# The head of a pooling and state-space decoder step: rows scaled in place before plain transposes, dt from the unsplit h, modulation in quarters, and a new order of loads and operations

## The chip, the cores and the metric

The kernel runs on one core of one Trainium2 chip. The time is that of one execution on the device, in microseconds (us), from the first to the last instruction of the core with what lies around it; a kernel's time is the median of its runs. All data are float32. Products that must be accurate are made as three passes over split numbers: an operand is split into a rounded high part (type fp32r) and the rest, the low part, and high x high, high x low and low x high are summed.

## The reference, cut to what matters

One layer of a hybrid decoder for 1024 prompt tokens and 8 x 8 sample tokens, 1088 rows in all. The change touches only the beginning:

```python
mod = jax.nn.silu(c) @ w_ada + b_ada                  # c: 1 prompt row + 8 sample rows
shift, scale, gate = jnp.split(mod, 3, axis=-1)       # 1024 each
h = rmsnorm(x, norm_g) * (1 + scale[:, None]) + shift[:, None]
proj = h @ w_in                                       # 1024 -> 8224 columns
u_pool, z_pool, z_ssm, xbc, dt_raw, g_raw = jnp.split(proj, SPLITS, axis=-1)
...                                                   # pooling, convolution, state space, gates
m = gates[..., :D_MODEL] * p + gates[..., D_MODEL:] * s
x = x + gate[:, None] * (m @ w_o)
```

`rmsnorm` divides each row of x by its root mean square. `w_ada` has 1024 x 3072 numbers: shift, scale and gate each take a third.

## The kernel before, in words

**The whole.** The projection h @ w_in is the first half of the program. After a head, columns come in 31 pairs of 128, each pair by one step of Strassen's scheme: seven products instead of eight, each of 24 matmuls (L595 to L597; two halves of 272 columns, four row blocks of the contraction, three passes). The state-space chunks and the output products follow, and a short tail of normalised output rows (L1954 to L1996). A program records instructions in an order written by hand; where `in_line` is called, that order is kept on every engine.

**The head (`first`, L838 to L999).** Its order is written out; engines take their instructions strictly in that order, and so does the queue of SyncE (SP), which issues nearly all loads.

1. The nine row blocks of x (128 rows each, 64 in the last) are loaded, then squared and summed (`x_square`; four on ScalarE, the 64 sample rows among them, five on VectorE), and 1/rms comes from a root and a reciprocal (`x_root`, `x_unit`). `x_unit` builds a diagonal matrix of 1/rms per block (L219).
2. `x_turn` (L223 to L233) multiplies each 128 x 128 piece of x by that diagonal matrix on TensorE (PE): the result is the piece turned and scaled, tokens along the free axis. There are 72 such products in ordinary float32, which the trace shows as two records each. `x_copy` brings them from PSUM into `tf[k]`, k = 0 to 7 being the eight blocks of 128 features. Tokens are cut in three blocks of 256, 384 and 448 columns, `BLK`, here called blocks 0, 1 and 2.
3. `ada_load`, `ada_mm`, `ada_out`, `ada_end`: the shift and scale thirds of w_ada (8 MB) are loaded in three parts (features k = 0 and 1, 2 and 3, and 4 to 7 of both), multiplied by silu(c) in four column groups of the array at once (L277), turned (L292) and finished with bias and norm weight into `md` (L296 to L299).
4. `h_make` (L309 to L335): from `tf[k]` and `md` it makes h in `tf[k]` itself (`L325` on ScalarE, `L327` on VectorE), its high part `hh_` (`L323`, `L332`, ScalarE) and low part `hl_` (`L315`, VectorE); the 64 sample columns have a shift and scale of their own (L330, L331, called the tail below).
5. `products`: the first pair of gate columns is made by plain three-pass products of h with two weight tiles of 512 columns' worth, loaded in halves (`w_first`: k < 4 and k >= 4), block by block (L866 to L868). `done` applies the sigmoid and stores the result.
6. `dt_block` (L720 to L731): the 32 columns of dt, as two sums, over the high and over the low parts of h, each in ordinary float32.
7. `gate_load`, `gate_mm`: the gate third of w_ada (4 MB, eight loads) for the end of the kernel; `gate_end` stores it.
8. `combine` (L471 to L519): the sums and differences of quarters of h for Strassen's scheme (S1 to S4), each split in high and low parts. The first pair of the scheme ("first pair" below) starts while these are being made.

**Buffers.** PSUM has 8 banks: three in pool `psA` (`PA`) and five in `psB` (`PB`). SBUF pools hand a buffer on when its last reader is done: 8 of tag `G` (blocks of w_ada, then h of k >= 4), 5 of `rawA` (scratch and raw weights of pairs), 3 of `raw`, 3 of `R`.

Of the kernel before, what the change touches and what calls it, by code (L numbers as in the profile page):

```python
# [20 lines left out]
P = 128  # L21
D = 1024
# [31 lines left out]
def tile_pool_ssd_step(  # L54
# [86 lines left out]

    c9 = const([P, KT, NB + 1], "c9")
# [42 lines left out]
    xr = []  # L185
# [4 lines left out]
    dg = []  # L190
# [3 lines left out]
    def x_load(i):  # L194
        n = P if i < 8 else NS
        xt = R([P, D]) if i == 8 else xbig[i // 4][:, i % 4, :D]
        load(xt[:n], x_prompt[0, i * P:(i + 1) * P, :] if i < 8 else x_sample.rearrange("b t d -> (b t) d"))
        xr.append((xt, n))
# [13 lines left out]
    def x_unit(a, b):  # L212
        n = xr[a][1]
        V.reciprocal(rs[:n, a:b], rs[:n, a:b])
        if not dg:
            dg.append(R())
        for i in range(a, b):
            n = xr[i][1]
            V.tensor_scalar(dg[0][:n, i * P:i * P + n], ident[:n, :n], rs[:n, i:i + 1], None, ALU.mult)  # L219
# [3 lines left out]
    def x_turn(g3, k):  # L223

        if g3 == 0:
            tf[k] = tfp.tile([P, T], F32, tag="tf", name=nm("tf"), bufs=8)
        px = PB()
        c = 0
        for i in range((0, *XG)[g3], XG[g3]):
            xt, n = xr[i]  # L230
            mm(px[:, c:c + n], xt[:n, k * P:(k + 1) * P], dg[0][:n, i * P:i * P + n], start=True, stop=True)
            c += n
        return g3, k, px, c  # L233
# [9 lines left out]
    def x_turns(g3, ks):  # L243
        for k in ks:
            x_copy(x_turn(g3, k), nc.scalar if k % 2 else V)


    PARTS = ((0, 2), (2, 4), (4, 8))
    pm, wraw, wtile = [None] * 3, {}, {}
    md = const([P, 16, 9], "md")  # L250

    def ada_load(part, k):
        a, b = PARTS[part]
        w = (b - a) * P
        if part == 0:
            if k == 0:
                wtile[0] = Y4(hp, F32)
            t = wtile[0][:, k // 2, :D]
        else:
            if part == 2 or k % 2 == 0:  # L260
                wtile[part, k] = G((P, D))
            t = wtile[part, k if part == 2 else k - k % 2]
        if part == 2:
            load(t, w_ada[8 + k])
        else:
            if k % 2 == 0:
                load(t, w_ada[4 * part + k // 2])
            t = t[:, k % 2 * 512:k % 2 * 512 + 512]
        wraw[part, k] = t.rearrange("p (s c) -> p s c", s=2)
# [17 lines left out]
    def ada_end(part, mr):  # L287
        a, b = PARTS[part]
        ni = (b - a) // 2
        ps = PB()  # L290
        for i in range(ni):
            nc.tensor.transpose(ps[:, i * P:(i + 1) * P], mr[:, i * P:(i + 1) * P], ident)  # L292
# [16 lines left out]
    def h_make(g3, ks):  # L309

        o, w = BLK[g3]
        e = min(o + w, SEQ) - o

        def low(k):
            V.tensor_tensor(hl_[k][:, o:o + w], tf[k][:, o:o + w], hh_[k][:, o:o + w].bitcast(F32), ALU.subtract)  # L315
        for k in ks:
            if hh_[k] is None:
                hh_[k], hl_[k] = h_tile(k, 0), h_tile(k, 1)
            t = tf[k][:, o:o + w]
            hi = hh_[k][:, o:o + w]  # L320
            sc, sh = md[:, 8 + k], md[:, k]
            if e == w:
                act(hi, t, AF.Identity, scale=sc[:, 0:1], bias=sh[:, 0:1])  # L323
            if k % 2:
                act(t[:, :e], t[:, :e], AF.Identity, scale=sc[:, 0:1], bias=sh[:, 0:1])  # L325
            else:
                V.tensor_scalar(t[:, :e], t[:, :e], sc[:, 0:1], sh[:, 0:1], ALU.mult, ALU.add)  # L327
            if e < w:
                ts_ = t[:, e:w].rearrange("p (b i) -> p b i", i=8)
                V.tensor_tensor(ts_, ts_, sc[:, 1:9].unsqueeze(2).to_broadcast([P, NB, 8]), ALU.mult)  # L330
                V.tensor_tensor(ts_, ts_, sh[:, 1:9].unsqueeze(2).to_broadcast([P, NB, 8]), ALU.add)  # L331
                act(hi, t, AF.Copy)  # L332
            if k > ks[0]:
                low(k - 1)
        low(ks[-1])  # L335


# [133 lines left out]
    def combine():  # L471
        L_, R_ = slice(0, HF), slice(HF, T)

        big = []

        def parts(src, hi, lo):
            act(hi, src, AF.Copy)
            V.tensor_tensor(lo, src, hi.bitcast(F32), ALU.subtract)

        def room(lst, k):  # L480
            if lst is S1:
                lst[k] = (hs.tile([P, 2, HF], F32R, tag="sq", name="S1", bufs=1) if k == 3 else R((P, 2, HF), F32R))
            else:
                if k == 0:
                    big.append(Y4(hs).rearrange("p k (j n) -> p k j n", j=2))
                lst[k] = big[-1][:, k]

        def part(lst, k, src):
            room(lst, k)
            parts(src, lst[k][:, 0], lst[k][:, 1])  # L490

        def low(k):
            V.tensor_tensor(S2[k][:, 1], tf[k][:, L_], S2[k][:, 0].bitcast(F32), ALU.subtract)
        for k in range(4):
            a, b = tf[k], tf[k + 4]
            room(S2, k)
            V.tensor_tensor(b[:, R_], a[:, R_], b[:, R_], ALU.add)
            V.tensor_tensor(a[:, R_], a[:, L_], a[:, R_], ALU.subtract)
            V.tensor_tensor(a[:, L_], b[:, R_], a[:, L_], ALU.subtract)
            act(S2[k][:, 0], a[:, L_], AF.Copy)  # L500
            if k:
                low(k - 1)
# [1579 lines left out]
```

## Time and profile before

| | |
|---|---|
| median of 3 runs | 1238.93 us (1238.75 to 1239.34) |
| profiled execution, span | 1238.8 us, clock 0.999 |
| PE busy | 1213.9 us, 98% |
| VectorE / ScalarE / GpSimd busy | 909.2 / 692.8 / 678.0 us |
| moved by DMA | 243.25 MB, mean 196 GB/s |

The profiled execution's own span, 1238.8 us, lies within 0.2 us of the median, so sums made in the trace stand for the time as they are. In the views, PE is TensorE, PEld its weight loads, DVE VectorE, ACT ScalarE, POOL GpSimd and SP SyncE; L231 is a line of the kernel before, and an idle time is followed by what ended it. PE records overlap (one ends after the next has begun), so the price of a matmul is the distance of two starts, not its length.

### The profile page before, as it was taken

How to read it: one execution, taken by the hardware profiler on the slowest of the kernel's cores; microseconds unless marked ns; L12 is line 12 of the kernel's file. 1: busy time of each engine (PE TensorE's matmuls, PEld its weight loads, DVE VectorE, ACT ScalarE, POOL GpSimd, SP SyncE). 2: the span in 40 equal slices, each digit the busy share in tenths (PEclk: the TensorE clock that was granted, in tenths of full speed). 3: DMA queues.
4: the chain of work that ended last, by engine and by line, in shares of the span. 5: the costliest groups of instructions: out<-in, count | busy, mean ns of one | idle time of the engine just before them, and what ended most of it. 6: DMA issues, size and time to landing. Idle time of an engine off the chain costs nothing. (4 is left out here: it accounts for less than half of the span.)

```text
span 1238.8 us, 25381 instructions
## 1 busy us (share of the span) xinstructions
PE 1213.9 (98%) x9364; PEld 1145.0 (92%) x9364; DVE 909.2 (73%) x1579; ACT 692.8 (56%) x1611; POOL 678.0 (55%) x555
## 2 busy tenths in 40 slices
PE   6999999999999999999999999999999999999997
PEld 6779999999999999999898899999999999999786
DVE  4796688985989588975867775787767879666543
ACT  4665356565566556554554454877877768432111
POOL 1006669768898877774444465364565557456000
PEclk9999999999999999999999999999999999999999
DMA  9726445755556554453877775998665676485431
GB/s 363 290 99 226 145 161 148 188 190 170 164 173 208 158 168 146 169 179 114 251 248 211 231 223 183 329 306 298 192 203 176 195 228 198 143 296 167 153 111 51
DMA packets 183916, 243.25 MB, mean 196 GB/s; under 512 B 40808, under 2 KB 116912, under 8 KB 183792
## 3 DMA queue, kind: packets, MB, share of 16 engines
q1 hardware_dynamic: 132128, 167.90, 42.9%
q10 hardware_dynamic: 51664, 73.72, 17.6%
q8 instruction: 74, 1.21, 0.4%
q14 instruction: 50, 0.41, 0.1%
HBM read 166.96 MB, written 74.62 MB: 195 GB/s over the span
## 5 line engine op out<-in xcount | busy, mean ns | idle before, releaser
L166 POOL TENSOR_TENSOR wlo<-rawA,whi 128x512 fp32r<-128x512 f32 x120 | 187.5, 1569 | 143.1 <-DVE wlo L166 67.7
L166 POOL TENSOR_TENSOR wlo<-raw,whi 128x512 fp32r<-128x512 f32 x92 | 150.2, 1640 | 126.1 <-ACT whi L163 119.9
L360 PE MATMUL mm<-Y,whi 128*128 128x352 f32 (+1 forms) x480 | 160.1, 334 | 0.6
L361 PE MATMUL mm<-Y,whi 128*128 128x352 f32 (+1 forms) x480 | 157.1, 327 | 0.4 <-DVE Y L1485 0.4
L362 PE MATMUL mm<-Y,wlo 128*128 128x352 f32 (+1 forms) x480 | 157.1, 327 | 0.0
L595 PE MATMUL mm<-Y,whi 128*128 128x272 f32 x496 | 144.5, 292 | 1.0 <-ACT whi L163 0.8
L597 PE MATMUL mm<-Y,wlo 128*128 128x272 f32 x496 | 143.5, 290 | 1.3 <-DVE wlo L166 0.8
L596 PE MATMUL ps<-Y,whi 128*128 128x272 f32 x496 | 143.2, 289 | 0.0
L595 PE MATMUL ps<-Y,whi 128*128 128x272 f32 x496 | 142.8, 288 | 0.0
L597 PE MATMUL ps<-Y,wlo 128*128 128x272 f32 x496 | 142.8, 288 | 0.0
L596 PE MATMUL mm<-Y,whi 128*128 128x272 f32 x496 | 142.5, 287 | 0.0
L1031 DVE SCALAR_TENSOR_TENSOR GA<-GA,cvT,GA 128x1112 f32<-128x1112 f32 x72 | 128.4, 1786 | 0.7 <-ACT GA L1028 0.5
L163 ACT ACTIVATE whi<-rawA 128x512 fp32r<-128x512 f32 x125 | 77.8, 626 | 90.4 <-PE ps L596 51.1
L163 ACT ACTIVATE whi<-raw 128x512 fp32r<-128x512 f32 x96 | 58.7, 626 | 83.0 <-DVE raw L540 38.2
L595 PEld LDWEIGHTS mm<-Y,whi 128*128 128x128 f32 x496 | 93.6, 189 | 4.6 <-issue 2.4
L597 PEld LDWEIGHTS mm<-Y,wlo 128*128 128x128 f32 x496 | 93.1, 188 | 3.0 <-DVE wlo L166 1.2
L595 PEld LDWEIGHTS ps<-Y,whi 128*128 128x128 f32 x496 | 93.4, 188 | 1.7 <-issue 0.8
L596 PEld LDWEIGHTS mm<-Y,whi 128*128 128x128 f32 x496 | 93.5, 188 | 0.8 <-issue 0.6
L360 PEld LDWEIGHTS mm<-Y,whi 128*128 128x128 f32 x480 | 90.2, 188 | 4.1 <-DVE G L1861 2.3
L596 PEld LDWEIGHTS ps<-Y,whi 128*128 128x128 f32 x496 | 93.3, 188 | 0.2
L597 PEld LDWEIGHTS ps<-Y,wlo 128*128 128x128 f32 x496 | 93.2, 188 | 0.0
L361 PEld LDWEIGHTS mm<-Y,whi 128*128 128x128 f32 x480 | 90.2, 188 | 2.6 <-DVE Y L1485 0.9
(422 smaller groups left out, 3727.0 us busy)
## 6 DMA issues: line engine op xcount, KB each, us to landing
rawA<-in_w_in SPq DMA_DIRECT2D x62, 512.0 KB
dec<-acs_d SPq DMA_DIRECT2D x32, 512.0 KB
xbc<-GA ACTq DMA_DIRECT2D x24, 512.0 KB
xb<-xbc SPq DMA_DIRECT2D x32, 384.0 KB
pw<-in_w_ssm_out ACTq DMA_DIRECT2D x32, 256.0 KB
ws<-ph ACTq DMA_DIRECT2D x32, 256.0 KB
ws<-pw SPq DMA_DIRECT2D x32, 256.0 KB
hs<-in_state_turned SPq DMA_DIRECT2D x32, 256.0 KB
```

The lines of the kernel that those rows point to most:

```text
L163: ins = act(hi[:, :, :ncols], raw[:, :, :ncols], AF.Copy)
L166: (eng or nc.gpsimd).tensor_tensor(lo[:, :, :ncols], raw[:, :, :ncols], hi[:, :, :ncols].bitcast(F32), ALU.subtract)
L360: mm(ps[:, :n], a, rh[k][:, o:o + n], start=(k == 0), stop=False)
L361: mm(ps[:, :n], a, rl[k][:, o:o + n], start=False, stop=False)
L362: mm(ps[:, :n], b, rh[k][:, o:o + n], start=False, stop=(k == nk - 1))
L595: mm(p, hi, ah, start=(k == 0), stop=False)
L596: mm(p, hi, al, start=False, stop=False)
L597: mm(p, lo, ah, start=False, stop=(k == 3))
L1031: V.scalar_tensor_tensor(d[:, :n], rp[:, k:k + n], cvT[:, 24 * k + mc:24 * k + mc + 1], d[:, :n], ALU.mult, ALU.add)
```

## The change

All of it is in the head; the instructions from the second pair on stand in the same order on every engine. In parts:

- `x_unit` no longer builds diagonal matrices. `x_scale` multiplies the rows of x by 1/rms in place (five blocks and the sample block on VectorE, three on ScalarE), and `x_turn` is a transpose against the identity. The sample block is filled to 128 rows with zeros and turned whole.
- 32 products of the identity with itself (`hot`) stand at the start of PE's order. ScalarE loads the root's table before it needs it. The sigmoid results go through `rawA` buffers.
- Shift and scale come in four parts of two features each.
- `h_make` is cut into single steps (`h_high`, `h_line`, `h_low`, `h_tail`, `h_copy`), some of which read PSUM directly; `combine` likewise. Four of the eight tail steps go to GpSimd, and so do three of the weight splits of the second half of the head and of the first pair.
- dt is made from h in `tf`, before the sums overwrite it: one sum instead of two.
- The order of everything in `first` is written out anew.
- The loads of the pooling weights and the loads of the next pairs' weights stand later in SP's order, and splits of the pairs that follow are held behind the last steps of the first pair's preparation (`tc.issue_after(held[...])`).

```diff
+    def x_scale(i, eng):
+        xt, n = xr[i]
+        if eng is None:
+            act(xt[:n], xt[:n], AF.Copy, scale=rs[:n, i:i + 1])
+        else:
+            eng.tensor_scalar(xt[:n], xt[:n], rs[:n, i:i + 1], None, ALU.mult)
...
-            mm(px[:, c:c + n], xt[:n, k * P:(k + 1) * P], dg[0][:n, i * P:i * P + n], start=True, stop=True)
+            nc.tensor.transpose(px[:, c:c + P], xt[:, k * P:(k + 1) * P], ident)
...
-    PARTS = ((0, 2), (2, 4), (4, 8))
+    PARTS = ((0, 2), (2, 4), (4, 6), (6, 8))
...
+    def h_line(g3, k, eng, src=None):
...
+        if eng is V:
+            V.tensor_scalar(t, u, sc, sh, ALU.mult, ALU.add)
+        else:
+            act(t, u, AF.Identity, scale=sc, bias=sh)
...
-    def dt_block(w, i):
+    def dt_mm(w, i):
         o, n = BLK[i]
-        ps = PA()
+        ps = dtp[i] = PA()
         for kk in range(2):
-            for part in (hh_, hl_):
-                for r in range(4):
-                    k = 4 * kk + r
-                    mm(ps[32 * r:32 * r + 32, :n], w[:, k, :], part[k][:, o:o + n].bitcast(F32),
-                       start=(kk == 0 and part is hh_), stop=(kk == 1 and part is hl_))
+            for r in range(4):
+                k = 4 * kk + r
+                mm(ps[32 * r:32 * r + 32, :n], w[:, k, :], tf[k][:, o:o + n], start=(kk == 0), stop=(kk == 1))
...
-            add(b11)
+            with tc.issue_after(held["act"]):
+                add(b11)
...
+        def hot(n):
+            for _ in range(n):
+                mm(banks[1, 0][:, :P], ident, ident, start=True, stop=True)
+
+        hot(20)
+        x_load(1)
+        x_load(0)
+        x_load(7)
...
-        x_turns(0, range(2))
...
+        products(1, range(7, 8))
...
+        next(opening, None)
+        sums_c(0)
...
```

On SP the loads at the start stand like this before (`Y_128` and `Y_129` hold x, `R_226` the sample rows, `Y_228` the first part of w_ada, `G_` the second, `raw_` the first halves of the first weights):

```order
L197 DMA Y_128<-in_x_prompt 128x1024 x4
L197 DMA Y_129<-in_x_prompt 128x1024 x4
L197 DMA R_226<-in_x_sample 64x1024
L267 DMA Y_228<-in_w_ada 128x1024 x3
L846 DMA raw_232<-in_w_first 128x512
L846 DMA raw_234<-in_w_first 128x512
L267 DMA Y_228<-in_w_ada 128x1024
L267 DMA G_237<-in_w_ada 128x1024
```

And after (`Y_129` and `Y_130` hold x, `R_245` the sample rows, `Y_248` the first part):

```order
L199 DMA Y_129<-in_x_prompt 128x1024 x2
L199 DMA Y_130<-in_x_prompt 128x1024 x3
L199 DMA R_245<-in_x_sample 64x1024
L258 DMA Y_248<-in_w_ada 128x1024 x2
L199 DMA Y_129<-in_x_prompt 128x1024
L199 DMA Y_130<-in_x_prompt 128x1024
L199 DMA Y_129<-in_x_prompt 128x1024
L258 DMA Y_248<-in_w_ada 128x1024 x2
L258 DMA G_256<-in_w_ada 128x1024
```

Two blocks of tokens of block 0 and the four of block 2 come first, two loads of w_ada are put ahead of the three row blocks of block 1, and the first weights come after the first part of w_ada.

Later on SP, the second halves of the first weights (`raw_578`, `raw_584`), the gate third (`R_`, `gk_`) and the last part of shift and scale (`G_574`, `G_580`) stand like this after; ahead of this piece are all of x, 14 blocks of w_ada's first two thirds and the two first halves:

```order
L789 DMA R_527<-in_w_ada 128x1024
L789 DMA R_529<-in_w_ada 128x1024
L258 DMA G_574<-in_w_ada 128x1024
L789 DMA R_576<-in_w_ada 128x1024
L818 DMA raw_578<-in_w_first 128x512
L258 DMA G_580<-in_w_ada 128x1024
L789 DMA gk_582<-in_w_ada 128x1024
L818 DMA raw_584<-in_w_first 128x512
L516 DMA rawA_586<-in_w_in 128x1024
L516 DMA rawA_588<-in_w_in 128x1024
L376 DMA cvT<-in_conv_vecs 128x120
```

Before, in the same place, the loads of the pooling weights (`pwt_`) stood between the two second halves (`raw_550`, `raw_552`), and the gate third came behind all of this:

```order
L846 DMA raw_550<-in_w_first 128x512
L748 DMA pwt_1290<-in_pool_w 128x128
L748 DMA pwt_2444<-in_pool_w 128x128
L748 DMA pwt_3919<-in_pool_w 128x128
L846 DMA raw_552<-in_w_first 128x512
L264 DMA G_554<-in_w_ada 128x1024
L264 DMA G_556<-in_w_ada 128x1024
L264 DMA G_558<-in_w_ada 128x1024
L264 DMA G_560<-in_w_ada 128x1024
```

The pooling weights left this place; four loads of the gate third moved ahead of the last weights.

On PE, at the end of the head, dt's products over high (`Y_463`, `G_727`) and low parts (`Y_464`, `G_728`, `G_733`) and the last four of the gate third stood right ahead of the first pair (L595):

```order
L727 MATMUL mm_955<-G_728,dtw 32x448
L727 MATMUL mm_955<-G_733,dtw 32x448
L823 MATMUL ps_794<-R_799,scT 32x256 x4
L823 MATMUL ps_794<-R_805,scT 32x256 x4
L823 MATMUL ps_794<-R_835,scT 32x256 x4
L823 MATMUL ps_794<-gk_841,scT 32x256 x4
L595 MATMUL mm_1009<-Y_463,whi_946 128x272
```

After, they read `tf` and stand among the products of blocks 1 and 2; the last of those (`ps_596`) now stand right ahead of the first pair (L563):

```order
L845 MATMUL ps_596<-G_863,whi_740 128x448
L846 MATMUL ps_596<-G_863,wlo_741 128x448
L847 MATMUL ps_596<-G_864,whi_740 128x448
L563 MATMUL mm_1064<-Y_490,whi_902 128x272
L564 MATMUL mm_1064<-Y_491,whi_902 128x272
L565 MATMUL mm_1064<-Y_490,wlo_903 128x272
```

What follows the first pair's first product on PE is a long row of like matmuls in both.

More of the change, by code (lines that the diff above doesn't have):

```diff
@@ new lines, in first @@
+        tt[1, 4] = x_turn(1, 4)
+        h_low(0, 0)
+        h_high(1, 1)
+        ada_mm(1, 3)
+        ada_load(3, 2)
+        gate_load(1)
+        gate_load(3)
+        w_lo(1, 0, V)
+        x_copy(tt[1, 5], nc.scalar)
+        ada_mm(1, 4)
+        x_copy(tt[1, 0], V)
+        products(0, range(0, 1))
+        h_copy(0)
+        h_line(1, 1, V)
+        h_high(1, 0)
+        ada_mm(1, 5)
+        h_low(2, 0)
+        ada_mm(2, 0)
+        x_copy(tt[1, 4], nc.scalar)
+        ada_mm(1, 6)
@@ new lines, in first @@
+        h_line(1, 0, V)
+        ada_mm(2, 1)
+        h_line(2, 1, None)
+        ada_mm(1, 7)
+        ada_load(3, 6)
+        gate_load(0)
+        w_load(1, 1)
+        ada_load(3, 4)
+        gate_load(2)
+        w_load(0, 1)
+        b11, b12, b21, b22 = light[0][0]()
+        for _ in late_loads():
+            pass
+        h_low(1, 1)
+        products(2, range(0, 1))
+        mr[1] = ada_out(1)
+        h_low(1, 0)
+        h_copy(1)
+        h_high(0, 1)
+        h_low(2, 1)
+        pt_[1] = ada_turn(1, mr[1])
@@ L958, in first @@
+        ada_mm(3, 5)
+        gate_mm(1)
+        h_high(0, 4)
+        h_low(2, 4)
+        ada_mm(3, 6)
+        h_high(1, 4)
+        gate_mm(2)
+        gate_load(6)
+        gate_load(5)
+        h_line(0, 4, V)
+        ada_mm(3, 7)
+        w_hi(0, 1)
+        h_low(0, 5)
+        gate_mm(3)
+        gate_load(7)
+        gate_load(4)
         dtw = dt_w()
-        run, (wz, wst) = light[0][1], light[0][0]()
         bg = gate_bias()
-        for k in range(4):
-            gate_load(k)
@@ L983, in first @@
-        dt_block(dtw, 2)
-        next(sums)
-        for k in range(4, 8):
-            gate_mm(k)
-        gate_end(bg)
-        next(late, None)
-        def hook(n):
-            if n in (0, 2):
-                next(wst)
-            if n < 2:
-                next(sums)
-            if n in (3, 4):
-                next(wst)
-                next(sums)
-        run(wz, hook)
+        h_low(0, 4)
+        h_line(1, 4, None)
+        products(1, range(2, 3))
+        w_lo(0, 1, V)
+        mr[3] = ada_out(3)
@@ new lines, in first @@
+        h_high(1, 7)
+        h_low(0, 6)
+        h_line(0, 7, V)
+        h_line(1, 6, None)
+        products(0, range(6, 7))
+        pw_diff(3)
+        h_line(1, 7, None)
+        products(1, range(5, 6))
+        h_low(0, 7)
+        h_copy(7)
+        h_low(1, 7)
+        h_line(2, 6, None)
+        products(0, range(7, 8))
+        h_low(1, 6)
+        h_low(2, 7)
+        pw_hi(0)
+        products(2, range(4, 5))
+        h_copy(6)
+        pw_lo(0, V)
+        done(0, 1)
+        h_low(2, 6)
```

579 lines of the change are left out of this document (368 added, 211 removed).

## The prediction

> **What bounds the kernel now.** I read the page's head first, then a table of windows whose cuts are places that the change touches. Its columns are the stretch, its length, the busy time (and records) of PE, PEld, DVE, ACT and POOL, the granted clock, the DMA share and GB/s.
>
> ```profile
> span 1238.8 us, 25381 instructions
> PE 1213.9 (98%) x9364; PEld 1145.0 (92%) x9364; DVE 909.2 (73%) x1579; ACT 692.8 (56%) x1611; POOL 678.0 (55%) x555
> ...
> 0.00:9.29 9.29, 0.00 (x0) 0.00 (x1) 2.97 (x7) 3.91 (x6) 2.37 (x30) 1.00 0.79 299
> 9.29:32.52 23.23, 23.15 (x209) 21.09 (x210) 12.12 (x33) 11.80 (x27) 2.75 (x3) 1.00 1.03 389
> 32.52:52.19 19.67, 19.09 (x204) 15.23 (x203) 12.96 (x36) 11.89 (x23) 0.00 (x0) 1.00 0.83 293
> 52.19:68.07 15.88, 14.91 (x104) 12.37 (x104) 14.02 (x33) 12.54 (x21) 0.00 (x0) 1.00 0.65 242
> 68.07:75.41 7.34, 7.34 (x97) 3.15 (x100) 7.13 (x12) 3.75 (x8) 0.00 (x0) 1.00 0.43 152
> 77.73:100.88 23.15, 21.92 (x168) 21.26 (x169) 21.49 (x35) 15.40 (x29) 3.62 (x3) 1.00 0.25 83
> 100.88:1200.00 1099.12, 1093.37 (x8390) 1043.57 (x8389) 822.13 (x1403) 624.67 (x1481) 667.20 (x518) 1.00 0.62 196
> ```
>
> From 100.88 us on, PE is busy in 1093 of 1099 us and nothing stands in another order. So time won before that point is handed on to the end nearly whole. Ahead of it PE is full as well, but with work that can shrink: 23.2 us from 9.29 us on go into turning x, 7.3 us (68.07 to 75.41) into dt. The first pair takes 23.15 us where the second takes 21.19 (row below), so it waits about 2 us. In the turning stretch DMA is full too (share 1.03, 389 GB/s), in the later ones it is not. What carries the kernel's end is therefore when the first pair starts (77.73 us) and how dense it runs.
>
> **The turns.** From the timelines of POOL and PE: the identity, the turning products cold and warm, and transposes made later in the kernel:
>
> ```profile
> 1.25 0.30 POOL masks.py:199 TENSOR_SCALAR_AFFINE_SELECT ident<-ident 128x128 f32<-128x128 f32 x1
> ...
> 9.29 4.42 PE L231 MATMUL ps<-R,Y 128*128 128x128 f32 x19 [9.29 <-DVE R L219]
> 13.71 6.86 PE L231 MATMUL ps<-R,Y 128*128 128x128 f32 x60
> ...
> 538.64 1.04 PE L1083 MATMUL ps<-ident,s 128*128 128x128 f32 x8
> 539.43 0.37 PE L595 MATMUL mm<-R,whi 128*128 128x272 f32 x1
> ```
>
> The 60 warm records stand 0.11 us apart, and a turning product has two: 0.22 us, 72 of them 16 us (with the sample pieces' narrow ones and the cold start some 20). Eight plain transposes take one record each and run from 538.64 to 539.5, 0.11 apart. So 72 transposes cost 7.8 us, some 8 us less on a full PE. By the Trainium skill, TensorE: Matmul & The Clock Gate, section Terms, the transpose mode is 4 times faster for float32, which would make it 4 us; the trace says 2 times, and I keep to the trace. Nothing in my sum would move by it, since PE will wait for loads there anyway.
>
> The scaling that takes the diagonal's place is nine operations of 1024 columns, on DVE and ACT. They come ahead of the transposes: first x1 and x0, so the first turn starts at 9 to 10 us as before, no gain. The 32 identity products stand in the first 10 us, which PE spends idle (9.29 us in the row above). At the cold distance of 0.23 us a record for 19 records and 0.11 after, 64 records take 9.4 us from the identity at 1.6 us: to 11 us, about 1 us past the first scaled row. That costs nothing if the copies out of PSUM, which need ACT, are later still; they are, as the scale of x0 and a root stand ahead of them.
>
> **What loads allow.** The sizes and the vector `md` before, from the views of DMA and the timeline:
>
> ```profile
> G<-in_w_ada SPq DMA_DIRECT2D x12, 512.0 KB
> Y<-in_x_prompt SPq DMA_DIRECT2D x8, 512.0 KB
> raw<-in_w_first SPq DMA_DIRECT2D x4, 256.0 KB
> ...
> 30.37 0.18 DVE L296 TENSOR_TENSOR md<-ps,vT 128x18 f32<-128x18 f32 x1 [1.43 <-PE ps L292]
> 50.97 0.20 DVE L296 TENSOR_TENSOR md<-ps,vT 128x36 f32<-128x36 f32 x1 [2.03 <-PE ps L292]
> ```
>
> The first part of shift and scale is there at 30.4 us before, although its loads (8 x blocks, the sample's half block, 4 of w_ada, two halves: 7.1 MB) were in by 9.29 + (7.1 - 2.8) / 0.389 = 20 us. PE was turning x until then. After, with 8 us of transposes, it follows its loads: about 22.5 us. The last part is there at 51 us before. After, the last load that products of k >= 4 need is the second half weight; 28 blocks of 0.524 MB and 5 half blocks stand up to it, 16.0 MB. 2.8 MB come in the first 9.29 us, the other 13.2 at 389 GB/s take 34 us: 43.3 us. A split on ACT and DVE (0.6 and 0.7 us, rows below) and hand-offs make it 45 us. This supposes that SP's queue never stands still for a buffer; I find each reused buffer's reader ahead of its load by some microseconds, but it is the sum's tightest assumption.
>
> **What PE, ACT and DVE must do by then.** Prices, PE by windows that hold one thing, ACT and DVE by groups:
>
> ```profile
> 34.09:35.98 1.89, 1.89 (x66) 1.69 (x65) 1.60 (x4) 0.98 (x2) 0.00 (x0) 1.00 0.23 42
> 53.66:56.63 2.97, 2.96 (x22) 2.68 (x23) 2.55 (x6) 2.90 (x6) 0.00 (x0) 1.00 0.80 327
> 57.63:62.02 4.39, 4.39 (x29) 4.14 (x25) 4.39 (x13) 2.44 (x5) 0.00 (x0) 1.00 0.66 243
> 62.02:63.02 1.00, 1.00 (x18) 0.42 (x17) 0.97 (x5) 0.60 (x2) 0.00 (x0) 1.00 0.00 0
> 63.02:68.07 5.05, 5.05 (x28) 4.42 (x24) 4.56 (x9) 4.16 (x7) 0.00 (x0) 1.00 0.70 237
> 100.88:122.07 21.19, 21.19 (x170) 21.11 (x169) 11.06 (x25) 11.40 (x25) 14.89 (x12) 1.00 0.71 241
> ...
> L325 ACT ACTIVATE tf<-tf,md 128x384 f32<-128x384 f32 x8 | 5.6, 701 | 0.1
> L332 ACT ACTIVATE G<-tf 128x448 fp32r<-128x448 f32 x4 | 2.3, 578 | 2.4 <-DVE tf L331 2.3
> L323 ACT ACTIVATE G<-tf,md 128x256 fp32r<-128x256 f32 x4 | 2.2, 591 | 1.8 <-DVE md L296 1.8
> L327 DVE TENSOR_SCALAR tf<-tf,md 128x384 f32<-128x384 f32 x8 | 3.8, 478 | 1.4 <-ACT G L323 1.0 <-ACT Y L323 0.4
> L315 DVE TENSOR_TENSOR Y<-tf,Y 128x384 fp32r<-128x384 f32 x4 | 2.2, 558 | 0.6 <-ACT tf L325 0.5
> ...
> L163 ACT ACTIVATE whi<-raw 128x512 fp32r<-128x512 f32 x8 | 4.8, 621 | 0.3 <-PE ps L596 0.3
> L166 DVE TENSOR_TENSOR wlo<-rawA,whi 128x512 fp32r<-128x512 f32 x5 | 3.3, 684 | 0.7 <-ACT whi L163 0.7
> ```
>
> A quarter of w_ada's two thirds costs PE 1.9 us, two k of the gate third 1.0, and products of four k 3.2 (block 0; 22 of its 24 matmuls are in 2.97), 4.4 (block 1) and 5.05 us (block 2), so 3.2 us for each k. From 22.5 us to the last weight PE has 24 transposes (2.6), three quarters (5.7), products of k < 4 without the last of block 1 (11.7), half the gate third (2.0) and turns of md (0.4): 22.4 us, to 44.9. Splitting the third part in two halves leaves its PE price as it was and lets k = 4 and 5 begin sooner. ACT has 38 operations in this stretch (12 of 384 at 0.70, 9 of 256 at 0.59, 6 of 448 at 0.58, five copies at 0.5, three splits at 0.6): 22 us by durations, somewhat less by starts. DVE has 48, nearly all between the 0.2 us of a tail and the 0.6 of a long low part: 20 us. Four tails on POOL are new there; as POOL takes 1.8 us for a split that DVE does in 0.7 (POOL's row stands below), a tail's two operations lie between 0.4 and 1.2 us there, ahead of one high part each. So loads, PE and ACT all come to about 45 us; three full queues that hand pieces to each other do not stay full. I allow 2 us of waits, two of the size of the longest before:
>
> ```profile
> PE mm L868 <- DVE G L315: 1.0, 1, 1.0
> PE mm L868 <- DVE Y L315: 0.4, 1, 0.4
> ```
>
> That puts the second half of the products at 47 us.
>
> **From there to the first pair.** PE has one product of block 1 (1.1), k = 4 to 7 (12.8), the other half of the gate third (2.0) and dt. Half of dt's matmuls go, those over the low parts, the rest have the same shape: 7.34 / 2 = 3.7 us. Together 19.6 us: the first pair starts at 66.6 us instead of 77.73.
>
> **The first pair.** Dense it takes 21.2 us. Before, it waited 2 us for splits. After, dt reads `tf`, so the sums can't overwrite it until the dt product of block 1 is done, at about 58 us (9 us before the pair starts); before, they ran beside dt. Behind that stand 38 operations of DVE, mostly these:
>
> ```profile
> 79.81 2.63 DVE L478 TENSOR_TENSOR Y<-tf,Y 128x544 fp32r<-128x544 f32 x4
> ...
> 97.15 2.46 DVE L478 TENSOR_TENSOR Y<-tf,Y 128x544 fp32r<-128x544 f32 x2
> 99.53 1.53 DVE L613 TENSOR_TENSOR u<-s,u 128x272 f32<-128x272 f32 x1
> 97.25 3.51 POOL L166 TENSOR_TENSOR wlo<-rawA,whi 128x512 fp32r<-128x512 f32 x2 [67.73 <-DVE wlo L166]
> ```
>
> Four of them start 0.64 us apart (2.63 less one's 0.72, by three), so 38 end near 83 us; the seventh product needs the last of them at 66.6 + 18 = 84.6. So DVE is 1 to 2 us from being late. Two splits of this pair go from DVE to POOL, and beside a POOL split DVE's operations stretched (the two of 97.15 take 2.46 us instead of 1.4): +1 us for each. I take 1.5 us of waits, so 22.7 us and an end at 89.3 us instead of 100.88: 11.6 us won. Bounds: no waits at all anywhere gives 85.8 us (15.1 won, a little more if the loads run above 389 GB/s); 5 us of waits in the first stretch and 6 in the pair give 96.8 (4.1 won).
>
> **What goes at nothing.** ACT's early root table hides in ACT's wait for x. The later loads of the next pairs' weights hide under the first pair. Sigmoids through other buffers, the later pooling weights and the zeros of the sample block lie beside PE's work; uncovered, each would be under 1 us.
>
> **The sum.** 1238.8 - 11.6 = 1227.2 us of span, 1227.3 as a time. A measurement here can tell about 0.2%, 2.5 us, from no change.
>
> **Rivals.** *The clock falls.* The 19 cold records stand 0.23 us apart against 0.11, for 4.4 us. If transposes with gaps for loads between 11 and 22 us do not keep the array warm, the transposes take twice as long and the next 4.4 us of real products half as much work: 2 to 3 us, partly under the loads, so 1229.5. For it: PE will idle some 4 us there. Against: ada products lie among the transposes, and no wait before 100 us in the trace shows a second cold stretch. The Trainium skill, TensorE: Matmul & The Clock Gate, Part 4, says that transposes do not count as busy for the clock; no run shown here tells. Chance 0.15.
>
> *DVE bounds the first pair.* If the DVE row of 38 is not dense (ACT's high parts stand between sums and low parts), S2, S1 and the last low parts each come late, in all 5 us instead of 1.5: 1231. Chance 0.17.
>
> *Every product waits for its h.* The order asks for h piece by piece: 24 groups of products each stand behind a fresh `h_high`, `h_line` and `h_low` on two engines. If each waits 0.97 us, as the one at 53.66 did, that is 23.3 us in place of my 2: 1248.6, slower. It decides for slower when the mean wait passes (11.6 + 2.5 + 2) / 24 = 0.67 us. Against it: before, most groups that had a lead of one piece waited for nothing, and ACT's and DVE's sums fit. Chance 0.07.
>
> *The gain is eaten by the second pair's weights.* Their loads stand behind the store of the gate rows now:
>
> ```profile
> 47.82 3.51 SPq L529 DMA_DIRECT2D rawA<-in_w_in  x3
> ...
> 82.81 1.37 SPq L835 DMA_DIRECT2D gate_d<-bg  x4
> ```
>
> Before they went out at 47.8 us; after at about 67 us at the earliest, behind `gate_end`, and their splits wait for the last step of the first pair's preparation (about 83 us), then take 1.8 us each on POOL. Needed: at 89.3 us. If loads or POOL slip by 10 us, the end is where it was: 1238. Chance 0.06.
>
> The forecast keeps 0.55. It and the two milder rivals make faster 0.87, with a share of the last rival 0.89; same 0.04, slower 0.07. The range runs from the no-wait bound, with loads a little faster, to the bound with 11 us of waits: 1221.5 to 1234.8.
>
> **What would show it.** In the changed profile: `md` first at 22 to 23 us, products of k >= 4 from 45 to 48 us, dt in 3.7 us, the first pair's first matmul at 64 to 69 us and 21.5 to 24 us long, DMA full to 43 us, PE's records 0.11 us apart throughout after 11 us, and the rest of the trace the same but shifted. A first pair at 77 us or later, or one of over 27 us, makes it wrong.

## The result, and the profile after

| | before | changed |
|---|---|---|
| median | 1239.34 us (1238.75 to 1240.38, 5 runs) | 1233.79 us (1231.92 to 1234.87, 5 runs) |
| ratio | | 0.995, 95% interval 0.9938 to 0.9962 |
| profiled execution: span, clock | 1238.8 us, 0.999 | 1232.0 us, 0.996 |

A second measurement gave 1232.63 us, beside 1240.56 us of the kernel before, and 0.9937 (0.9923 to 0.995). So the change wins 5.5 to 8 us, where 11.6 was forecast. The time lies 1.7 to 1.8 us above the span in nearly every run (1233.79 and 1232.0 in the profiled one). What "Time and profile before" says of the two is therefore wrong: the profiled span of 1238.8 us stands for about 1240.5 us of time, somewhat above the median.

The page's head of the changed kernel, then its table of windows, with the columns of the prediction's table:

```profile
span 1232.0 us, 25396 instructions
PE 1212.0 (98%) x9372; PEld 1146.3 (93%) x9372; DVE 908.6 (74%) x1564; ACT 696.0 (56%) x1621; POOL 685.9 (56%) x565
```

```profile
12.66:20.14 7.48, 6.85 (x64) 5.48 (x64) 6.64 (x13) 6.56 (x16) 0.00 (x0) 1.00 1.03 410
20.14:22.07 1.93, 0.01 (x1) 0.01 (x1) 1.72 (x4) 1.85 (x3) 0.00 (x0) 1.00 1.02 397
22.07:27.30 5.23, 4.71 (x73) 4.09 (x74) 0.69 (x1) 1.50 (x4) 0.00 (x0) 0.67 1.03 406
27.30:45.00 17.70, 17.70 (x236) 15.14 (x238) 14.19 (x41) 15.69 (x32) 2.83 (x7) 1.00 1.03 405
45.00:57.29 12.29, 11.56 (x125) 9.69 (x115) 9.80 (x23) 10.69 (x20) 2.00 (x4) 1.00 0.66 220
57.29:68.21 10.92, 10.92 (x103) 7.80 (x103) 8.47 (x13) 7.46 (x14) 0.00 (x0) 1.00 0.22 77
68.21:91.66 23.45, 21.70 (x170) 21.21 (x168) 22.26 (x35) 13.33 (x26) 6.59 (x4) 1.00 0.61 207
1070.00:1085.00 15.00, 15.00 (x92) 14.78 (x92) 3.58 (x9) 4.16 (x12) 2.36 (x1) 0.89 0.80 287
```

The cuts are the first turn (12.66 us), PE's wait for the third step of the first quarter (20.14 to 22.07), the first `md` (27.30), dt (57.29), and the first pair (68.21 to 91.66). From the first `md` to the first pair PE stands still once, 0.72 us ahead of dt. The first pair starts 9.5 us earlier than before (77.73) and ends 9.2 us earlier (100.88). In the pair DVE is busy in 22.26 of 23.45 us. The granted clock is 0.67 from 22.07 to 27.30 us and 0.89 around 1075: in two stretches PE runs at half clock, which the profile of the kernel before does not show there. In PE's timeline the first of them looks like this:

```profile
22.07 0.86 PE L268 MATMUL ps<-Y,scT 128*32 128x128 f32 x24 [1.93 <-DMA Y<-in_w_ada]
...
25.74 1.42 PE L235 MATMUL ps<-ident,Y 128*128 128x128 f32 x6
...
27.10 0.82 PE L235 MATMUL ps<-ident,Y 128*128 128x128 f32 x6
```

Six transposes take 1.26 us, up to the turn at 27.00 us, 0.21 apart; six more from 27.10 us stand 0.11 apart. Half clock lasts from about 23.5 to 26.9 us, 3.4 us; half of that, 1.7 us, is my estimate of its price. Of PE's waits (us in total, times, longest) these three matter. The prediction had expected waits for loads here and some in the pair, but not a late first turn:

```profile
PE ps L268 <- DMA Y<-in_w_ada: 2.6, 2, 1.9
...
PE mm L565 <- DVE wlo L895: 1.5, 1, 1.5
...
PE ps L235 <- ACT Y L221: 1.4, 1, 1.4
```

The last is the first turn's, at 12.66 us. The timelines of DVE and ACT show the chain ahead of it: on DVE three squares from 6.79 us on (the third is not needed yet), then the reciprocal and the scaling of x1; ACT scales x0 only from 11.47 us, behind a square of x5 that waited for its load.

```profile
6.79 1.23 DVE L206 SCALAR_TENSOR_TENSOR sqj<-Y 128x1024 f32<-128x1024 f32 x1
...
10.42 0.75 DVE L223 TENSOR_SCALAR Y<-Y,rs 128x1024 f32<-128x1024 f32 x1
...
11.47 1.13 ACT L221 ACTIVATE Y<-Y,rs 128x1024 f32<-128x1024 f32 x1
```

### The profile page after: what moved, and what is told of

The parts are those of the page before. It is cut to its first block, busy times and chain, and to the rows that moved or that the text cites. A ratio compares the mean times of both kernels' runs of the same rounds, so it can differ in the third digit from the quotient of the medians.

```text
span 1232.0 us, 25396 instructions
## 1 busy us (share of the span) xinstructions
PE 1212.0 (98%) x9372; PEld 1146.3 (93%) x9372; DVE 908.6 (74%) x1564; ACT 696.0 (56%) x1621; POOL 685.9 (56%) x565
## 5 line engine op out<-in xcount | busy, mean ns | idle before, releaser
L167 POOL TENSOR_TENSOR wlo<-rawA,whi 128x512 fp32r<-128x512 f32 x120 | 190.2, 1590 | 87.9 <-ACT whi L164 67.9
L563 PE MATMUL mm<-Y,whi 128*128 128x272 f32 x496 | 144.3, 291 | 0.3 <-DVE GA L581 0.3
L563 PE MATMUL ps<-Y,whi 128*128 128x272 f32 x496 | 142.9, 288 | 0.0
L164 ACT ACTIVATE whi<-rawA 128x512 fp32r<-128x512 f32 x120 | 74.8, 626 | 88.2 <-PE ps L564 45.7
L164 ACT ACTIVATE whi<-raw 128x512 fp32r<-128x512 f32 x90 | 55.3, 627 | 88.1 <-DVE raw L527 47.4
L563 PEld LDWEIGHTS mm<-Y,whi 128*128 128x128 f32 x496 | 93.6, 189 | 3.3 <-issue 2.6
L563 PEld LDWEIGHTS ps<-Y,whi 128*128 128x128 f32 x496 | 93.4, 188 | 1.7 <-issue 0.8
```

The costliest lines, as they stand in the source:

```text
L164: ins = act(hi[:, :, :ncols], raw[:, :, :ncols], AF.Copy)
L167: (eng or nc.gpsimd).tensor_tensor(lo[:, :, :ncols], raw[:, :, :ncols], hi[:, :, :ncols].bitcast(F32), ALU.subtract)
L563: mm(p, hi, ah, start=(k == 0), stop=False)
```

## The experiments

My theory after the result: PE's work between the first turn and the first pair shrank by the forecast amounts (8 us of turning, 3.7 us of dt), and the lead was then lost in four pieces: waits for loads, half clock, a late split in the first pair, and something after 91 us. Rivals stand with each run. Times compare with 1233.8 and 1232.6 us of the changed kernel; medians of one kernel differ by 1 to 1.6 us between measurements, so the traces decide between small terms.

### The parts of the change

**Turning by products again**, with the scaling in place kept:

```diff
-            nc.tensor.transpose(px[:, c:c + P], xt[:, k * P:(k + 1) * P], ident)
+            mm(px[:, c:c + P], xt[:, k * P:(k + 1) * P], ident, start=True, stop=True)
```

> The turns of x are products with the identity again (two records each) with x still scaled in place; all else as in the changed kernel. Theory: 72 more records at 0.11 us are 7.9 us on PE; 3.1 us of it fall into waits for loads (0.63 + 1.93 + 0.52) and the cold spell of 1.7 us goes, so the first pair starts 3.1 us later, at 71.3 us, and the time is 1236.9. Rival A (the gain comes from the new order of loads, not from the transposes): time 1233.8, within 0.6. Rival B (nothing hides): 1241.7.

Measured: 1237.67 us, ratio 0.9983 (0.9973 to 0.9993); first pair at 72.36 us.

**dt from both parts of h again** (the 24 matmuls over `tf` become 48 over `hh_` and `hl_`).

> dt is taken from the high and low parts of h again (48 products instead of 24), all else as in the changed kernel. Theory (PE is full there): 3.7 us more of PE ahead of the first pair, which starts at 71.9 us; the first pair's stall of 2.3 us at its fourth product shrinks by up to 1.5 us, since the sums run beside a longer dt: time 1236.0 to 1237.5. Rival (DVE's row of sums and low parts sets the end of the first pair, so halving dt only moved the wait): the pair ends at 91.7 us as in the changed kernel and the time is 1233.8.

Measured: 1236.03 us, 0.9969 (0.9957 to 0.998); first pair at 70.67 us. The window from the first turn to the first pair, in the changed kernel, with turning by products, and with dt from both parts:

```profile
12.66:68.21 55.55, 51.74 (x589) 42.20 (x589) 41.50 (x94) 43.76 (x86) 4.83 (x10) 0.97 0.79 300
```

```profile
13.74:72.36 58.62, 57.82 (x660) 49.49 (x661) 41.24 (x94) 44.33 (x86) 4.70 (x10) 1.00 0.73 279
```

```profile
12.61:70.67 58.06, 53.78 (x637) 42.33 (x637) 41.66 (x94) 43.85 (x86) 4.79 (x10) 1.00 0.74 287
```

PE's busy time is 51.74 us less 1.7 of half clock, 50.0 (a run below without half clock has 50.4); with turning by products 57.8, with the old dt 53.8. So transposes save about 7.8 us and dt about 3.8, as forecast. Of the 7.8 only 4.15 reach the first pair: turning by products has 0.8 us of waits in place of 3.8 and no half clock, and its first turn comes 1.1 us later. With the old dt the first pair starts only 2.5 us later, not 3.7, since half clock is missing there too, and the longest wait in the pair does not shrink, though the theory said it would: 1.5 us as in the changed kernel. The rivals fall, the loads' order alone gains nothing like 5 us, and 3.9 to 5.0 us of time for the transposes and 2.2 to 3.4 for dt add up to about the whole gain.

**The two operations in the old order.** Into the kernel before: rows scaled in place, transposes, dt from `tf` with its three blocks ahead of the sums that overwrite `tf`. Of the edit, the part on the order:

```diff
-            next(sums)
-        dt_block(dtw, 0)
-        dt_block(dtw, 1)
-        next(sums)
-        next(wst)
-        dt_block(dtw, 2)
-        next(sums)
+        for i in range(3):
+            dt_block(dtw, i)
+        for _ in range(4):
+            next(sums)
+        next(wst)
+        next(sums)
```

> The kernel before with the two cheaper operations alone: rows of x scaled in place (nine operations in turn on DVE and ACT) and turned by plain transposes, and dt from unsplit h, its three blocks ahead of the sums, since these overwrite what dt reads. Loads, shift and scale in three parts and the order of the rest stay; no identity products ahead. Theory (the gain is 11.6 us less work on a full PE, less what loads and DVE then ask for; the new order only arranges it): turning ends at 25 us, md at 23 to 25 us, first pair at 68 to 70 us, with a stall of 2 to 4 us at its fourth product, since the sums start behind dt; time 1233 to 1235.5. Rival (the order is what turns less work into time): PE waits for loads and pieces, first pair at 73 us or later, time 1236.5 or more.

Measured: 1245.35 us, 1.0042 (1.0029 to 1.0055): slower than before, and my theory fell. Windows, then lines of the timelines of DVE, ACT and PE of that kernel:

```profile
20.36:27.00 6.64, 6.29 (x64) 5.31 (x64) 2.00 (x5) 3.49 (x6) 1.11 (x1) 0.50 1.03 412
27.00:72.17 45.17, 42.85 (x428) 32.34 (x420) 27.82 (x73) 28.92 (x52) 1.65 (x3) 1.00 0.76 284
72.17:81.72 9.55, 0.00 (x1) 0.00 (x0) 9.26 (x14) 4.26 (x8) 0.00 (x0) 0.64 0.16 58
```

```profile
70.46 0.72 DVE L500 TENSOR_TENSOR tf<-tf,tf 128x544 f32<-128x544 f32 x1 [6.64 <-PE mm L729]
...
81.06 1.14 ACT L163 ACTIVATE whi<-rawA 128x512 fp32r<-128x512 f32 x2
...
81.72 0.59 PE L598 MATMUL mm<-Y,whi 128*128 128x272 f32 x1 [9.55 <-ACT whi L163]
```

PE has done its work at 72.17 us, although half clock held it back (0.50 from 20.36 to 27.00 us), 5.6 us before the first pair started in the kernel before, and then stands still for 9.55. DVE had waited 6.64 us for dt (L729), since the sums may not touch `tf` sooner. What ends PE's wait is the high split of the pair's first weights on ACT (L163): it stands behind ACT's high parts of the sums, and so behind eleven microseconds of sums on DVE. In the changed kernel the splits of the first two weights stand ahead of the sums, and DVE waits for dt only 1.02 us there. So the order is no decoration: it turns less work on PE into time. An old order with only those splits moved was not tried.

**Without the 32 identity products** (`hot(20)` and `hot(12)` left out).

> The changed kernel without its 32 identity products. Theory (PE waits 1.9 us for a load at 20 to 22 us anyway): the first turns run at half clock for about 3.4 us, which takes up that wait; md at 27 us or earlier, first pair at 67 to 68.5 us, time 1232.5 to 1234.5. Rival A (they keep the clock up through the head): cold records until 18 us and again after the wait, time 1235.5. Rival B (they hold back the first turn, as PE is busy with them to 11.3 us): first turn at 11 us or earlier, first pair 1 us earlier, time 1232.8.

Measured: 1231.88 us, 0.9934 (0.9919 to 0.9948); `md` at 25.37, first pair at 67.15 us. PE's timeline:

```profile
12.80 1.94 PE L235 MATMUL ps<-ident,Y 128*128 128x128 f32 x8 [12.80 <-ACT Y L221]
...
18.23 0.85 PE L235 MATMUL ps<-ident,Y 128*128 128x128 f32 x3
...
20.85 0.49 PE L235 MATMUL ps<-ident,Y 128*128 128x128 f32 x3
```

Three transposes take 0.64 us to the next row at 18.23 us and 0.33 at 20.85; between them the clock comes up, at 19.2 us by the trace's record of it. Turning at half clock fills the time until the load is there at 22 us, PE does not wait for it, and no half clock follows. The theory holds, and the identity products bring nothing: without them the median is 0.8 to 1.9 us lower, within the spread of the runs. The granted clock of the views reads 1.00 at the slow start all the same: that column does not show the first rise.

### The head: what sets the first md

**The vectors' operation behind the first squares** (`v_turn()` moved behind `x_scale(1, V)`).

> The one operation of DVE that waits for the small vectors (6.69 us in the changed kernel) stands behind the scaling of x1 instead of ahead of the first square. Theory (the first md waits for the last w_ada block of the first quarter, which lands at 22.07 us, so the late first turn costs nothing): first square near 4.6 us, first turn at 11.3 us (behind the identity products) instead of 12.66, PE's wait before 22.07 us longer by as much, md still at 27.3 us, first pair at 68.2 us, time within 0.6 us of the changed kernel's 1233.8. Rival (the late first turn is what made the head 1.6 us later than forecast): md at 25.9, first pair at 66.8 us, time 1232.4.

Measured: 1231.92 us, 0.9935 (0.9922 to 0.9948). The first square starts at 6.45 us, as soon as its load is there, instead of 6.79, and the first turn at 13.16: not that operation held the first turn, but the loads. So the edit did not bring the earlier first turn that would test the rival directly. The trace speaks against it: PE still waits 2.08 us for the same load, which is there at 22.70 us instead of 22.07, and `md` comes 3.63 us behind it, at 26.33 us (5.23 us behind it in the changed kernel, with 1.7 of half clock). The first pair comes at 67.44 us although the first turn is later, because the half clock is missing in this stretch. Of the theory the part stands that a late first turn costs nothing.

**Two blocks of w_ada ahead of three of x.**

```diff
-        x_load(3)
-        x_load(4)
-        x_load(2)
         ada_load(0, 4)
         ada_load(0, 2)
+        x_load(3)
+        x_load(4)
+        x_load(2)
```

with the root, the scaling and the turns of these blocks behind `ada_end(0, ...)`.

> The last two w_ada blocks of the first quarter are loaded ahead of the three x blocks of the middle token block, and the steps of the quarter, its copy, turn and end stand ahead of that block's scaling and turning; the rest as in the changed kernel. Theory (PE is full from the first md on, so the first md sets the first pair): md at 23 us instead of 27.3 us, first pair at 64.5 to 66 us instead of 68.2, as the last half weight lands at 43 us; time 1230 to 1231.5. Rival (DVE and ACT, 80 and 89 per cent busy from 27 to 45 us, hand the pieces over no sooner): md earlier, PE with new waits between 25 and 45 us, first pair at 68 us, time 1233.8.

Measured: 1235.03 us, 0.9966 (0.9955 to 0.9977). `md` comes at 24.50 us, but the first pair at 68.55. The longest of PE's waits up to 70 us, and the stretch from the first turn to the first pair:

```profile
PE ps L235 <- DVE Y L223: 1.8, 1, 1.8
...
13.39:68.55 55.16, 50.43 (x589) 40.79 (x590) 42.75 (x97) 42.94 (x84) 5.55 (x10) 1.00 0.78 300
```

PE now waits for the middle block's scaling. The theory, that the first `md` sets the first pair, fell. What sets it is simpler: PE has 50 us of work from the first turn to the first pair whatever its order, and every wait or half clock in that stretch is added (here 50.4 us busy and 4.7 idle). Until about 22 us PE can only be as far as the loads are, and DMA is full (shares of 1.02 to 1.03). The profiled execution, 1232.84 us, is the fastest of twelve (up to 1239.03), so what slows the others does not show here.

**Eight identity products in PE's wait** (`hot(8)` ahead of `ada_mm(0, 2)`).

> Eight more identity products (16 records, 1.8 us) stand ahead of the third step of the first w_ada quarter, in PE's wait of 1.93 us for a load. Theory (the granted clock falls from 23.45 to 26.9 us because PE stood still before; the spell costs 1.7 us): records 0.11 us apart throughout from 22 us, md at 25.6 us instead of 27.3, first pair at 66.5 us, time 1.7 us under the changed kernel's: 1232.1. Rival A (it is the long row of transposes, which the clock does not count as work; 1.8 us of products are too little): the cold spell stays, time 1233.8. Rival B (the spell is hidden, since loads bind later): md earlier, first pair at 68.2 us, time 1233.8.

Measured: 1235.76 us, 0.9965 (0.9954 to 0.9977), 2 to 3 us slower than the changed kernel. Its windows behind two of PE's waits:

```profile
15.00:19.00 4.00, 4.00 (x31) 3.19 (x32) 4.00 (x8) 2.59 (x7) 0.00 (x0) 0.57 1.03 410
...
79.19:83.30 4.11, 4.11 (x22) 4.11 (x23) 4.01 (x8) 3.07 (x7) 0.00 (x0) 0.65 0.27 106
```

The wait at 20 us is filled and no half clock follows it, but one came earlier, behind the wait for the first turn (10.79 to 13.20 us), one in the first pair, behind its stall (77.70 to 79.19), and a third at 1077 us. `md` comes at 26.82 and the first pair at 67.76 us. So warming one gap was no cure. Why the median is worse by more than one such stretch (1.7 us) is open.

### The first pair

**The fourth product's low weights sooner** (`pw_lo(3, V)` moved from behind `parts_lo(S3, 0, ...)` to behind `sums_c(1)`).

> The low part of the fourth product's weights is made on DVE right behind the sums, where DVE waited 1.1 us for ACT, instead of behind six low parts of the activations; all else as in the changed kernel. Theory (the pair's stall is this one operation's place): the fourth product takes 3.5 us or less instead of 5.3, with at most 1 us of new waits in the fifth to seventh, so the pair lasts 22.2 to 22.7 us instead of 23.45, and the time is 1232.5 to 1233.0. Rival (DVE's whole row sets the pair's end): a later product takes the wait over, the pair lasts 23.4 us, time 1233.8.

Measured: 1230.93 us, 0.9929 (0.9917 to 0.9942). The pair in a window and its waits:

```profile
68.40:91.25 22.85, 21.83 (x170) 21.20 (x169) 22.26 (x35) 13.36 (x26) 6.56 (x4) 1.00 0.60 215
```

```profile
PE mm L563 <- DVE u L576: 0.6, 1, 0.6
```

The fourth product takes 3.53 us instead of 5.29, but the sixth 4.18 instead of 3.03: it waits for a sum that stands behind the same row. 0.6 us is won in the pair, as DVE is busy in 22.26 of 22.85 us. That is the rival in kind, smaller in size. The profiled span is 2.5 us shorter than the changed kernel's; of that some 1.3 us lie in no half clock at 1075 us.

**Three edits together**: that one, `pw_lo(5)` and `pw_lo(6)` on POOL, and the shift of the next part.

> The changed kernel with three edits: tiles 32 bytes further on (an unused column of constants), the low part of the fourth product's weights made right behind the sums, and the low parts of the sixth and seventh product's weights on POOL, which is idle there, instead of DVE. Theory: 1.1 us from the addresses, 0.6 us from the fourth product's weights, and about 1.2 us more in the first pair, since DVE's row is then 1.4 us shorter: the pair lasts 21.4 to 22 us, time 1230.0 to 1231.0. Rival (POOL's splits stretch DVE's operations beside them): the pair lasts 22.9 us, time 1231.5.

Measured: 1231.68 us, 0.9935 (0.9922 to 0.9947); the pair lasts 23.59 us, with 4.58 us in the fourth and 3.88 in the sixth product. Beside two splits on POOL instead of one, DVE's six low parts take 6.10 us where the changed kernel's take 5.00: the rival holds, and by more than it said (22.9 us); what DVE is relieved of it loses again. No version here is clearly better than the changed kernel: the intervals overlap. The nearest to it is the single edit before this one, with five of its six times below all ten of the changed kernel, but measured on another chip.

### After the first pair

**Tiles 32 bytes further on.** The change adds one column of constants, for the root of epsilon, ahead of most tiles of the kernel. One such column alone moves 1067 of the 1713 tiles of the kernel before by 32 bytes (h and the weights of the pairs among them); the others, `tf` and the state-space tiles among them, are laid out from the other end of SBUF and stay. One more unused column moves the tiles by 32 again:

```diff
     eps_root = const([P, 1], "eps_root")
+    const([P, 1], "pad")
```

> The changed kernel with one more unused column of constants behind the new one, so that every later tile lies 32 bytes further on, at the same place within 64 bytes as in the kernel before; no instruction differs. Theory (the new column for the root of epsilon moved every tile by 32 bytes, and the rate of some products hangs on it): the lead over the kernel before no longer falls by 1.0 us between 813 and 1058 us and by 0.9 us between 1159 and 1225 us, and no longer rises by 1.0 us at about 680 to 706 us; in sum 0.9 us faster than the changed kernel, 1232.9. Rival (addresses do not matter; the drift belongs to the run or the chip): the lead drifts as it did, time 1233.8.

The same unused column alone, in the kernel before:

> The kernel before with one unused column of constants at the place of the changed kernel's new one: all later tiles lie 32 bytes further on; no instruction differs. Theory (alignment): against the kernel before it gains about 1.0 us at 680 to 706 us and loses 1.0 us between 813 and 1058 us and 0.9 us between 1159 and 1225 us, in sum 0.9 us slower. Rival: the same times at every place, no drift.

Measured: 1231.3 us, 0.9936 (0.9922 to 0.9951), and 1241.42 us, 1.0021 (1.0009 to 1.0032). In DVE's timelines the same four instructions, first of the kernel before, then of the same with the column, then of the changed kernel, then of that with the column:

```profile
813.57 0.69 DVE L1444 TENSOR_TENSOR v<-v,sz 128x512 f32<-128x512 f32 x1
...
1058.18 0.68 DVE L1452 TENSOR_TENSOR hst<-hst,ps 128x512 f32<-128x512 f32 x1
...
1158.48 1.29 DVE L1975 TENSOR_TENSOR R<-ps,G 128x512 f32<-128x512 f32 x2 [5.80 <-DMA G<-gate_d]
...
1226.67 0.69 DVE L1975 TENSOR_TENSOR R<-ps,G 128x512 f32<-128x512 f32 x1 [0.49 <-PE ps L1974]
```

```profile
811.88 0.68 DVE L1445 TENSOR_TENSOR v<-v,sz 128x512 f32<-128x512 f32 x1
...
1057.45 0.68 DVE L1453 TENSOR_TENSOR hst<-hst,ps 128x512 f32<-128x512 f32 x1
...
1157.31 1.29 DVE L1976 TENSOR_TENSOR R<-ps,G 128x512 f32<-128x512 f32 x2 [5.58 <-DMA G<-gate_d]
...
1226.77 0.69 DVE L1976 TENSOR_TENSOR R<-ps,G 128x512 f32<-128x512 f32 x1 [0.59 <-PE ps L1975]
```

```profile
803.44 0.68 DVE L1692 TENSOR_TENSOR v<-v,sz 128x512 f32<-128x512 f32 x1
...
1049.01 0.68 DVE L1700 TENSOR_TENSOR hst<-hst,ps 128x512 f32<-128x512 f32 x1
...
1150.36 1.29 DVE L2223 TENSOR_TENSOR R<-ps,G 128x512 f32<-128x512 f32 x2 [5.53 <-DMA G<-gate_d]
...
1219.85 0.69 DVE L2223 TENSOR_TENSOR R<-ps,G 128x512 f32<-128x512 f32 x1 [0.59 <-PE ps L2222]
```

```profile
801.88 0.68 DVE L1693 TENSOR_TENSOR v<-v,sz 128x512 f32<-128x512 f32 x1
...
1046.79 0.67 DVE L1701 TENSOR_TENSOR hst<-hst,ps 128x512 f32<-128x512 f32 x1
...
1146.36 1.29 DVE L2224 TENSOR_TENSOR R<-ps,G 128x512 f32<-128x512 f32 x2 [5.42 <-DMA G<-gate_d]
...
1215.70 0.69 DVE L2224 TENSOR_TENSOR R<-ps,G 128x512 f32<-128x512 f32 x1 [0.58 <-PE ps L2223]
```

From the first to the second row it takes 244.61, 245.57, 245.57 and 244.91 us, from the third to the fourth 68.19, 69.46, 69.49 and 69.34. With no instruction changed, 32 bytes cost the kernel before 0.96 and 1.27 us: that is shown. A further 32 bytes give 0.66 us of the first back and nearly none of the second, which the theory did not foresee. In the first stretch ten profiles with one such column show 245.56 to 245.58 us, two with the addresses of before 244.61, and two with the further column 244.91 and 244.92. In the second the two with the addresses of before show 68.17 and 68.19 us, all others 69.2 to 69.6. The gain at 680 to 706 us is no matter of addresses: the old order with the two operations, which has the addresses of before, shows 1.2 us of it too, so the profiled execution of the kernel before lost it there. Which operands and which boundary count stays open.

**The changed kernel once more.**

> The changed kernel once more, unchanged. Theory (stretches of 3.4 us at half clock follow some of PE's idle or narrow stretches, and which of them is chance of the run): the profile shows its spells at other places than 23.4 to 26.9 us and 1075 to 1078 us or leaves one out; first pair between 66.5 and 68.5 us accordingly, time 1232 to 1235. Rival (the spells belong to the kernel's order): both spells at the same places.

Measured: 1232.63 us, 0.9937 (0.9923 to 0.995). Three windows of this execution, then two of the first:

```profile
23.07:26.48 3.41, 3.41 (x64) 2.91 (x64) 0.69 (x1) 0.63 (x1) 0.00 (x0) 0.50 1.03 406
...
77.68:81.10 3.42, 1.71 (x12) 1.28 (x11) 3.42 (x7) 0.82 (x3) 0.00 (x0) 1.00 0.54 214
81.10:84.51 3.41, 3.41 (x17) 3.41 (x16) 3.31 (x6) 2.35 (x6) 0.00 (x0) 0.50 0.21 82
```

```profile
78.10:81.51 3.41, 1.93 (x15) 1.85 (x15) 3.41 (x8) 1.07 (x3) 0.00 (x0) 1.00 0.36 145
81.51:84.93 3.42, 3.42 (x30) 3.42 (x29) 3.31 (x7) 2.01 (x5) 0.00 (x0) 1.00 0.29 105
```

Half clock at 23 us again, none at 1075 us, and one in the pair instead, behind a stall of 1.48 us that the first profile has as well and that cost nothing more there. So one and the same kernel gets a stretch or not, as the theory said. What decides can be read off: in all fourteen profiles of this case the granted clock changes only at whole multiples of 3.413 us from its own first rise (6.00 us here, 6.42 in the first profile), and the windows above are steps of that grid. Here the stall and what lies around it leave PE busy for 1.71 us of one step, and the next step runs at half clock; in the first profile they leave 1.93 us, and the clock stays.

Half clock falls behind three kinds of places: waits in the turning, the pair's stall, and the 18 products of one column at 1071.73 us, where PE counts as busy but the array has little to do:

```profile
1071.73 2.05 PE L2053 MATMUL ps<-ones,sq_acc 128*128 128x1 f32 x18
...
1075.23 0.52 PE L364 MATMUL mm<-Y,whi 128*128 128x384 f32 x1
```

The matmul of 1075.23 us is 0.32 us ahead of the next of its kind; 0.17 is usual. In four of the fourteen profiles all 1.98 us of the narrow products lie within one step of the grid, and these four have half clock behind them; in the other ten the end of a step cuts them, at most 1.86 us lie in one, and the clock stays. The pair's stall brings half clock in three of the nine profiles that have it in full, those with PE busy for 0.49 to 0.50 of the step, and not in the six with 0.55 or more. In the head the border is less sharp: four steps with PE busy for 0.46 to 0.49 were followed by full clock, two with 0.50 by half clock. So what looks like chance is mostly how the grid, which starts at the first rise, falls on the kernel's waits.

## Why the prediction was right in kind and too large

- **Turns and dt**: right. 0.11 us a record, 7.8 us (8 forecast); dt 3.8 us (3.7).
- **The first turn** at 9 to 10 us "as before, no gain": wrong, 12.66 us, but free by the trace, since PE waits for a load at 20 us in any case. That the identity products cost next to nothing fits the run without them.
- **The first `md`** at about 22.5 us: wrong, 27.3 us. The load that it needs came at 22.07 us and not at 20, six steps and a turn still follow, and half clock took 1.7 us. The rival "The clock falls" came true here in part, in both profiles of the changed kernel: the transposes up to 20 us ran at full clock, 0.11 us apart, and the fall came behind the wait for the load. The Trainium skill, TensorE: Matmul & The Clock Gate, Part 4, says that transposes do not count as busy; without the identity products the clock rose at 19.2 us, after 6.4 us of turning with only two steps of ordinary products among them, so here they seem to count.
- **The first pair** at 66.6 us: 68.21. DMA was full until about 45 us (43.3 forecast), and products of k >= 4 began at 48.60 us (47 forecast). From `md` on I had priced 42.1 us of work and 2 of waits; it was 40.2 and 0.7. Three full queues did stay full, and products did not wait for their h: that rival is out. So of 4.8 us only 1.6 remained.
- **The pair in 22.7 us**: 23.45. "DVE bounds the first pair" was right in kind and too dear in price: 2.25 us of waits instead of 1.5 or 5. The second pair started without a wait at 91.66 us, so the rival of its weights is out too.
- **"Time won before 100.88 is handed on to the end nearly whole"**: this is the step that failed. The lead is 9.2 us at the pair's end, 10.1 at 803 us, 9.2 at 1049, 8.1 at 1150 and 6.8 at 1220 us (differences of the rows above). The addresses took 2.2 us of it, the stretch from 1049 to 1150 us with its half clock 1.0 (the second profile, without half clock there, lost nothing), and 0.9 had come from the profile of before. "The rest of the trace the same but shifted" did not hold.
- **The sum**: 1227.2 us of span was 1232.0: 1.6 in the first pair's start, 0.75 in its length, 2.4 after it. The time stands 1.7 us above the span, which I had left out. Together that is 6.5 us, from 1227.3 to 1233.8. That the time still lies inside the range is partly luck: its upper end, 1234.8 us, stands for 11 us of waits in the head and the first pair, and most of what was lost lies elsewhere, in the clock, the addresses and the 1.7 us.

## What to carry to other kernels

Price the work that a full engine loses, but take from it the waits that open where loads arrive no sooner; here half of the turning's 7.8 us went there and into half clock. On an engine that is otherwise full, a wait of 1.5 to 2.4 us can cost up to 1.7 us more behind it, when half clock follows. Before an operand of a long-running operation is overwritten later than before, look at what stands behind the overwriting operation on its engine: in the old order that alone cost more than the whole gain. And when a kernel's untouched part gets slower, compare the addresses: one added constant moved most of the tiles and cost the kernel before 2.2 us in two stretches, 1.4 us of its median.

## What of the hardware was not expected

- Shifting most SBUF tiles by 32 bytes changed 245 us of unchanged instructions by 0.96 us, and 68 us by 1.27.
- PE ran at half clock for 3.4 us behind waits of only 1.5 to 2.4 us, and behind 1.98 us of one-column products without any wait, in some executions and not in others, by how they lay on a grid of 3.413 us. The Trainium skill, TensorE: Matmul & The Clock Gate, Part 1, has a free-running window of about 3.4 us and asks for an idle window; the length and the grid agree, but here much less than a whole window of idleness was enough (PE busy for 0.28 to 0.50 of it).
- From 9 to 11 us DMA's share was 1.10 at 268 GB/s in the changed kernel, against 1.02 at 407 from 13 to 16 us. The kernel before has its dip from 13 to 16 us, 1.04 at 288. In both it lies about where the load of the 64 sample rows stands in the queue; that this load is the cause was not tested.
